# One Strassen step in the input projections of a hybrid attention and state-space layer

## The chip, the cores and the metric

The kernel runs on one core of one Trainium2 chip, as a single launch. The metric is its device time in microseconds (us). Three runs of the kernel before were timed, and one further execution was recorded by the hardware profiler. A difference between two kernels is the ratio of such times.

## The reference, cut to what matters

One layer is computed for a new stream of 2048 tokens and for 32 sample tokens that continue another stream. All data are fp32, the model width is 1024.

```python
h = _rms_norm(x, pre_norm_w)
proj = h @ w_in                       # 1024 x 9760 columns
q, k, v, g_att, z, xbc, dt_raw, gate_a, gate_s = _split_cols(proj)
q, k = rope(q), rope(k)
att = windowed attention of q, k, v with sinks
branch_a = (att * silu(g_att)) @ w_attn_o
xs, bm, cm = split(silu(causal_dwconv(xbc, conv_buf, conv_w, conv_b)))
dt = softplus(dt_raw + dt_bias)
y, h_new = chunked state-space scan of xs, dt, bm, cm from state h0   # the state is carried on
yz = y * silu(z)
yz = group-wise RMS norm of yz, 4 groups of 512
branch_s = yz @ w_ssm_o
merged = sigmoid(gate_a) * branch_a + sigmoid(gate_s) * branch_s
out = x + _rms_norm(merged @ w_out, post_norm_w)
```

The columns of `w_in` are 1024 for q, 256 each for k and v, 1024 for the attention gate, 2048 for z, 3072 for x, B and C (the input of the convolution), 32 for dt, and 1024 for each of the two merge gates.

## The kernel before

The 2048 tokens are worked through in four blocks of 512; block 1 also takes the 32 sample tokens, 544 in all. Activations lie transposed, channels on the 128 partitions and tokens along the row, so a projection's result tile is 128 output channels by the block's tokens.

**A job.** One job is one such tile of one projection. The weight tile (1024 x 128) is split into two fp32r parts, hi (ScalarE copies it, L131) and lo (VectorE subtracts hi from the weight, L135), and so are the activations (`hhi`, `hlo`, made in `stage_a`, L262 and L263). A job adds up 24 matmuls (L151): for each of 8 slices of 128 input channels hi x hi, hi x lo and lo x hi, each 512 columns in one PSUM bank, or two times 272 in block 1. The PSUM pool `mm` has four banks for this. A function `evac` of the job then takes the result from PSUM.

**The weights.** In block 0 each weight tile is read, split, and the two parts are kept in DRAM (`wd`, L137); blocks 1 to 3 read them from there (L126). `prep` runs two jobs ahead of the matmuls (`LOOK`), loads in block 0 four (`LOOK_DMA`). The tiles of the pool `wp` hold them.

**Order.** The jobs of a block are listed in a fixed order: dt; then for each of the four groups of the scan four tiles of x, one each of B and C, four of z, and the state projection (`ssm_out`, 8 half-length jobs) of the group two before it, which stands between x and B; then K, V, and Q and attention gate in turns, 8 + 8 merge gate tiles, the attention's output projection and the output. Four stages can be told apart in block 0: scan 30 to 395 us, attention 395 to 560, merge gates 560 to 660, output projections to 755. Block 1 runs from 755 to 1535, block 2 from 1540 to 2279 (its scan stage to 1935), block 3 to 3006.

**Side work.** What isn't a projection is a list of steps: scan chunks, norms, attention units, the next block's `stage_a`. One step is issued per full job (the counter `units_`), so that its instructions stand between matmuls in TensorE's queue. A job may name steps that have to be through before it (`need`); they are then issued at once.

**Parts that the change touches.** `evac_conv` (L370 and on) copies a tile from PSUM with a halo (L381), applies four taps, one on ScalarE (L384) and three on VectorE (L387), and SiLU (L393). `silu2` (L402, L403) makes the gate z from PSUM. A chunk of the scan loads its cumulated sums (L422, L425), prepares (decay tile `rr` at L447, `s`, `xh`, `xl` at L461 to L466 on GpSimd and ScalarE) and finishes (L477 to L496; `H` is the carried state, all in SBUF). `squares` and `norm` follow the last chunk. RoPE (L627 to L630), the splits of Q (L699, L700) and of K (L726, L728) into hi and lo, and the scores (L765, L766) are in the attention part. `emit_first` (L154) emits dt and the first two tiles half by half in block 0, so that they start before the second half of the activations is there. All DMAs are issued by SyncE (SP).

## Time and profile before

| | us |
|---|---|
| median of three runs | 3019.72 (3015.81 to 3024.2) |
| profiled execution | 3019.91 |
| its span in the trace | 3018.1 |
| TensorE busy | 2969.7 |
| VectorE busy | 1733.8 |
| ScalarE busy | 1128.8 |
| GpSimd busy | 502.7 |

The profiled execution is 1.8 us longer than its span, and 0.2 us from the median of the runs. The granted clock of TensorE was 0.998 of full speed over the span, which is its upper level of 2.4 GHz. Busy time is that of matmuls (PE), weight loads (PEld) and of the instructions of VectorE (DVE), ScalarE (ACT) and GpSimd (POOL); waits on semaphores are not in it.

### The profile page before, as it was taken

The page shows a single profiled execution, that of the slowest core. Times are in us where ns is not written, and L with a number is a line of the kernel's source. Part 1 is how long each engine was busy: PE and PEld are TensorE (multiplying, and loading weights), DVE is VectorE, ACT ScalarE, POOL GpSimd, SP SyncE. Part 2 cuts the span into 40 slices and gives each one's busy share as a digit, 9 for nine tenths or more (in the row PEclk, how much of TensorE's full clock was granted, in tenths as well). Part 3 has the DMA queues.
Part 4 walks back from the last instruction along what each step waited for, and adds up shares of the span by engine and source line. Part 5 has one row for each costly group of instructions (what it writes and reads, how often), then busy time and mean ns, then how long its engine had stood idle before and what let it go on. Part 6 is the DMA issues. An engine that isn't in the chain of part 4 may idle for free.

```text
span 3018.1 us, 46690 instructions
## 1 busy us (share of the span) xinstructions
PE 2969.7 (98%) x17983; PEld 2527.1 (84%) x17983; DVE 1733.8 (57%) x3722; ACT 1128.8 (37%) x2752; POOL 502.7 (17%) x599
## 2 busy tenths in 40 slices
PE   8999999999999999999999999999999999999998
PEld 7877877788999999999998877887788777887787
DVE  6878777644686756563346745655135766556402
ACT  5655435433454323342124433234123443124311
POOL 1322210001132312000102222200011222110000
PEclk9999999999999999999999999999999999999999
DMA  8977786697756455334557555543657665554454
GB/s 283 286 252 255 265 269 223 207 304 266 230 178 182 148 191 173 140 120 182 203 181 235 178 193 187 189 154 126 216 211 228 201 189 172 192 173 153 156 200 155
DMA packets 306214, 606.99 MB, mean 201 GB/s; under 512 B 21768, under 2 KB 231016, under 8 KB 258888
## 3 DMA queue, kind: packets, MB, share of 16 engines
q1 hardware_dynamic: 305992, 604.00, 60.4%
q8 instruction: 142, 2.33, 0.3%
q14 instruction: 80, 0.66, 0.1%
HBM read 478.86 MB, written 125.09 MB: 200 GB/s over the span
## 4 chain that ended last, share of the span: by engine, by line
PE 56%; DVE 4%; DMA 3%; ACT 2%; issue 1%; POOL 1%; SPq 0%; DVEq 0%; POOLq 0%; ACTq 0%
PE mm L151 49%; DMA rr<-cd 2%; PE sd L804 1%; PE sd L787 1%; PE sd L481 1%; DVE u L387 1%; PE sd L477 1%; PE sd L765 1%; PE sd L485 1%; PE sd L766 1%; ACT rr L450 1%; DMA w<-wd 1%; POOL rr L447 1%; PE sd L446 0%; PE sd L920 0%
## 5 line engine op out<-in xcount | busy, mean ns | idle before, releaser
L151 PE MATMUL mm<-hhi,w 128*128 128x512 f32 (+2 forms) x6160 | 1673.6, 354 | 2.4 <-DMA w<-wd 1.3
L151 PEld LDWEIGHTS mm<-hhi,w 128*128 128x128 f32 x6160 | 1082.6, 188 | 167.0 <-issue 12.1
L151 PE MATMUL mm<-hlo,w 128*128 128x512 f32 (+2 forms) x3104 | 1091.0, 352 | 0.4 <-DVE hlo L263 0.4
L151 PEld LDWEIGHTS mm<-hlo,w 128*128 128x128 f32 x3104 | 586.0, 189 | 75.6 <-DVE hlo L263 0.7
L151 PE MATMUL mm<-u,w 128*128 128x512 f32 (+1 forms) x2880 | 567.6, 353 | 0.2 <-DMA w<-wd 0.2
L151 PEld LDWEIGHTS mm<-u,w 128*128 128x128 f32 x2880 | 467.3, 188 | 76.6 <-issue 2.8
L450 ACT ACTIVATE rr<-rr,ncum 128x128 f32<-128x128 f32 (+1 forms) x544 | 170.0, 386 | 131.7 <-POOL rr L447 131.5
L387 DVE SCALAR_TENSOR_TENSOR u<-xp,par,u 128x512 f32<-128x512 f32 (+1 forms) x240 | 172.8, 743 | 43.9 <-ACT u L384 43.4
L135 DVE TENSOR_TENSOR w<-raw,w 128x1024 fp32r<-128x1024 f32 (+1 forms) x124 | 147.1, 1187 | 64.9 <-ACT w L131 64.4
L151 PE MATMUL mm<-tA,w 128*128 128x512 f32 (+2 forms) x688 | 174.0, 340 | 0.1
L743 ACT ACTIVATE pt<-sd,nm 128x192 f32<-128x192 f32 (+3 forms) x260 | 105.2, 413 | 156.9 <-DVE nm L737 142.1
L889 POOL TENSOR_TENSOR s<-s,S 128x512 f32<-128x512 f32 (+1 forms) x32 | 45.4, 1417 | 636.3 <-DVE s L888 601.6
L131 ACT ACTIVATE w<-raw 128x1024 fp32r<-128x1024 f32 (+1 forms) x125 | 118.5, 948 | 62.5 <-PE mm L151 46.4
L629 POOL TENSOR_TENSOR s<-s,cs 128x512 f32<-128x512 f32 (+1 forms) x40 | 52.7, 1318 | 467.4 <-DVE s L627 467.4
L151 PEld LDWEIGHTS mm<-tA,w 128*128 128x128 f32 x688 | 118.3, 188 | 14.2 <-ACT tA L892 0.3
L888 DVE SCALAR_TENSOR_TENSOR s<-tA,mm 128x512 f32<-128x512 f32 (+1 forms) x40 | 23.4, 584 | 182.7 <-PE mm L151 182.7
L381 ACT COPY xp<-mm 128x512 f32<-128x512 f32 (+1 forms) x120 | 59.1, 493 | 175.9 <-PE mm L151 172.3
L447 POOL TENSOR_SCALAR_AFFINE_SELECT rr<-rr 128x1024 f32<-128x1024 f32 (+1 forms) x68 | 84.1, 1237 | 232.9 <-DMA rr<-cd 207.3
L735 DVE TENSOR_REDUCE mx<-sd 128x2 f32<-128x384 f32 (+3 forms) x140 | 66.0, 511 | 88.7 <-PE sd L766 82.1
L151 PE MATMUL mm<-S,w 128*128 128x512 f32 (+2 forms) x344 | 116.4, 338 | 0.4 <-DVE S L893 0.4
L403 DVE SCALAR_TENSOR_TENSOR u<-s,mm 128x512 f32<-128x512 f32 (+1 forms) x80 | 46.4, 586 | 116.0 <-ACT s L402 116.0
L580 DVE TENSOR_TENSOR S<-S,mm 128x512 f32<-128x512 f32 (+1 forms) x120 | 69.6, 585 | 72.9 <-PE mm L151 72.6
(245 smaller groups left out, 3637.6 us busy)
## 6 DMA issues: line engine op xcount, KB each, us to landing
w<-wd SPq DMA_DIRECT2D x276, 1024.0 KB
wd<-w SPq DMA_DIRECT2D x92, 1024.0 KB
w<-wd SPq DMA_DIRECT2D x99, 512.0 KB
raw<-in_w_in_dram SPq DMA_DIRECT2D x77, 512.0 KB
rr<-cd SPq DMA_DIRECT2D x64, 512.0 KB
wd<-w SPq DMA_DIRECT2D x33, 512.0 KB
ee<-cd SPq DMA_DIRECT2D x128, 128.0 KB
x<-in_x_prompt_dram SPq DMA_DIRECT2D x24, 512.0 KB
```

What stands on the lines that cost most here:

```text
L131: act.activation(hi, src, AF.Copy)
L135: vec.tensor_tensor(lo, src, hi.bitcast(F32), op=ALU.subtract)
L151: last_mm[0] = pe.matmul(ps, w[:, k, :], r(k, n0, n), start=k == 0 and i == 0, stop=k == kt - 1 and i == len(ops) - 1)
L381: act.copy(xp[:, 3 + n0:3 + n0 + m], ps[:, :m])
L387: vec.scalar_tensor_tensor(o[:, d0:d0 + n], xp[:, off + t:off + t + n], convw[:, t, ci:ci + 1], o[:, d0:d0 + n], op0=ALU.mult, op1=ALU.add)
L403: vec.scalar_tensor_tensor(o[:, n0:n0 + n], t[:, n0:n0 + n], 1.0, ps, op0=ALU.add, op1=ALU.mult)
L447: pl.affine_select(w[:q, :, :q], w[:q, :, :q], pattern=[[0, 8], [1, q]], compare_op=ALU.is_ge, fill=-1e30, base=0, channel_multiplier=-1)
L450: act.activation(w[:q, h, :q], w[:q, h, :q], AF.Exp, scale=1.0, bias=ncum[:q, co + g * 8 + h:co + g * 8 + h + 1])
L580: vec.tensor_tensor(s[:, n0:n0 + n], s[:, n0:n0 + n], ps, op=ALU.add)
L629: pl.tensor_tensor(sh[:, :tb], sh[:, :tb], cs[:, 1, :tb], op=ALU.mult)
L735: vec.tensor_reduce(mx[:, cols], src, axis=AX.X, op=ALU.max)
L743: act.activation(dst, src, AF.Exp, bias=nm[:, i:i + 1], scale=0.125, accum_out=den[:, i:i + 1])
```

## The change

Two neighbouring 128-column tiles of an input projection become one pair. The 1024 input channels are cut in two halves (A11, A12 are the pair's first column tile, A21, A22 its second), and the tokens of the block in two halves (B11, B21 the two channel halves of the first tokens, the others of the second). One Strassen step in Winograd's form makes the four result tiles from seven products in place of eight. Each product is 4 channel slices x 3 matmuls (hi x hi, hi x lo, lo x hi) of 256 columns, 272 in block 1. 38 pairs a block take this path; the state projection, the attention output and the output projection stay as they are.

- **Activations:** `stage_a` makes the sums t1 to t4 beside the block's B11, B21 and B22 (`sums_a`, `sums_b`, `sums_c`) and splits all of them.
- **Weights:** three of a pair's seven weight pieces are blocks of the weight itself, loaded and split in every block (in block 0 the subtraction is on VectorE, in blocks 1 to 3 on GpSimd). The other four are sums, added on GpSimd in block 0, split on VectorE and kept in DRAM. `wp` has nine slots for pieces and four for raw blocks; `supply` runs eight pieces ahead.
- **Results:** `emit_pair` takes each product from PSUM into the two result tiles in SBUF: products 0 and 4 by a ScalarE copy, the other five by VectorE, with two half-width sums on GpSimd behind product 4. Convolution, SiLU, RoPE and gates then read SBUF.
- **dt** is five half-block products of 8 matmuls, and `emit_first` is gone.
- **z** goes to DRAM (`zd`) and is read back and multiplied on behind the scan, in `squares`, which is now two steps on its own.
- **The carried state** goes through DRAM between blocks (`hstate`); the pool `u` has 2 tiles, not 5, `rr` 2, not 3.
- **Q and K** stay plain fp32 for the scores, four matmuls a unit on row halves.
- **Side work** advances two steps a pair (`tick`), and the state projection comes ahead of the group's x.

Lines that only rename, `add_entries`, `group`, `spread`, and the changes to RoPE and the output of blocks 0 to 2 are left out here.

```diff
-LOOK = 2
-LOOK_DMA = 4
+NW = 9
+NR = 4
...
-    wp = pool("wp", 3)
+    wp = pool("wp", NW)
     hp = pool("hp", 1)
-    up = pool("up", 5)
+    up = pool("up", 2)
     sp = pool("sp", 8)
     s2 = pool("s2", 6)
+    xq = pool("xq", 2)
...
-    hhi = hp.tile([P, KT, UW], F32R, name="hhi")
-    hlo = hp.tile([P, KT, UW], F32R, name="hlo")
+    HN = UW // 2
+    hb = {n: hp.tile([P, 2, HK, HN], F32R, name=n) for n in ("b11", "b21", "b22", "t1", "t2", "t3", "t4")}
+    hstate = [wdram.tile([P, 512], F32, name=f"hst{g}") for g in range(4)]
...
+    def load_raws():
+        while rawnext[0] < min(len(rawlist), rawdone[0] + NR):
+            i = rawnext[0]
+            view, k0, c0 = rawlist[i]
+            r = wp.tile([P, HK * P], F32, name="raw", bufs=NR)
+            dma(r.rearrange("p (k c) -> p k c", k=HK), view[:, k0:k0 + HK, c0:c0 + P])
+            rawtiles[i] = r
+            rawnext[0] += 1
+
...
+    def halves(w, src, eng):
+        act.activation(w[:, 0], src, AF.Copy)
+        eng.tensor_tensor(w[:, 1], src, w[:, 0].bitcast(F32), op=ALU.subtract)
...
+        if not first and kind != "pure":
+            n = 1 if kind == "mix" else 2
+            dma(w[:, :n].bitcast(F32), held[e % per_block[0]])
             return
...
+        elif kind == "plain":
+            halves(w, rawtiles[en["raw"]], vec)
+            keep(e, w)
+            raw_free()
+        elif not first:
+            halves(w, rawtiles[en["raw"]], pl)
+            raw_free()
         else:
-            vec.tensor_tensor(lo, src, hi.bitcast(F32), op=ALU.subtract)
-        held[j] = wdram.tile([P, used.shape[1]], F32, name=f"wd{j}")
-        dma(held[j], used.bitcast(F32))
+            r11, r21, r22, r12 = (rawtiles.get(en["raw"] + i) for i in range(4))
+            pos = en["pos"]
+            if pos == 0:
+                halves(w, r11, vec)
+            elif pos == 1:
+                s1 = s2.tile([P, UW], F32, name="s2")[:, :HK * P]
+                pl.tensor_tensor(s1, r21, r22, op=ALU.add)
+                pl.tensor_tensor(r21, r21, r11, op=ALU.add)
+                pl.tensor_tensor(r11, r11, s1, op=ALU.add)
+                en["s1"] = s1
+                halves(w, r11, vec)
+                keep(e, w)
+            elif pos == 2:
+                halves(w, r12, vec)
+                pl.tensor_tensor(r12, r12, r11, op=ALU.add)
+                raw_free()
...
+            elif pos == 4:
+                halves(w, entries[e - 3]["s1"], vec)
+                keep(e, w)
+            elif pos == 5:
+                halves(w, r22, vec)
+                raw_free()
...
+    def supply():
+        while nalloc[0] < min(len(entries), nused[0] + NW - 1):
+            alloc(nalloc[0])
+            nalloc[0] += 1
...
+    def emit_dt(j):
+        jb = jobs[j]
+        n = jb["tb"] // 2
+        e0, e1 = jb["entries"]
+        res = []
+
+        def run():
+            for n0, ops in ((0, ((e0, "b11"), (e1, "b21"))), (n, ((e0, "t3"), (e0, "b22"), (e1, "b22")))):
+                ps = mm.tile([P, 512], F32, name="mm")[:, :n]
+                for i, (e, h) in enumerate(ops):
+                    yield from group(ps, e, moving(h, n), 0, n, i == 0, i == len(ops) - 1)
+                res.append((ps, n0, n))
+        spread(run(), 5 * HK * 2)
+        used(2)
+        jb["evac"](res)
+
+    def emit_pair(j, between):
+        jb = jobs[j]
+        tb = jb["tb"]
+        n = tb // 2
+        es = jb["entries"]
+        y0, y1 = jb["dest"]()
+        first, second = slice(0, n), slice(n, tb)
+
+        def run(which):
+            for i in which:
+                ps = mm.tile([P, 512], F32, name="mm")[:, :n]
+                name = ("b11", "t2", "b21", "t3", "t1", "t4", "b22")[i]
+                yield from group(ps, es[i], moving(name, n), 0, n, True, True)
+                used(1)
+                if i == 0:
+                    act.copy(y0[:, first], ps)
+                elif i == 1:
+                    vec.tensor_tensor(y0[:, second], ps, y0[:, first], op=ALU.add)
+                elif i == 2:
+                    vec.tensor_tensor(y0[:, first], ps, y0[:, first], op=ALU.add)
+                elif i == 3:
+                    vec.tensor_tensor(y1[:, first], ps, y0[:, second], op=ALU.subtract)
+                elif i == 4:
+                    act.copy(y1[:, second], ps)
+                    pl.tensor_tensor(y0[:, second], y0[:, second], y1[:, second], op=ALU.add)
+                    pl.tensor_tensor(y1[:, second], y1[:, first], y1[:, second], op=ALU.subtract)
+                elif i == 5:
+                    vec.tensor_tensor(y1[:, first], ps, y1[:, first], op=ALU.add)
+                elif i == 6:
+                    vec.tensor_tensor(y0[:, second], ps, y0[:, second], op=ALU.add)
+        spread(run((0, 1, 2)), 9 * HK)
+        between()
+        spread(run((3, 4, 5, 6)), 12 * HK)
+        for f, y in zip(jb["evac"], (y0, y1)):
+            f(y)
...
+    def add_pair(view, c1, c2, tb, dest, evacs, **kw):
+        a11, a12, a21, a22 = ((view, k0, c) for c in (c1, c2) for k0 in (0, HK))
+        es = add_entries("pure", [a11, None, a12, None, None, a22, None], [a11, a21, a22, a12])
+        new_job(dict(kind="pair", entries=es, tb=tb, dest=dest, evac=evacs, **{k: list(v) if k != "name" else v for k, v in kw.items()}))
...
+            def sums_a():
+                r = st["rawh"]
+                if b > 0:
+                    parts("b11", "b11")
+                vec.tensor_tensor(r["b11"], r["b11"], r["t1"], op=ALU.subtract)
+                vec.tensor_tensor(r["t1"], r["t1"], r["b22"], op=ALU.subtract)
+
+            def sums_b():
+                r = st["rawh"]
+                parts("t3", "t1")
+                if b > 0:
+                    parts("b22", "b22")
+                    parts("b21", "b21")
+                vec.scalar_tensor_tensor(r["b22"], r["b11"], -1.0, r["b22"], op0=ALU.mult, op1=ALU.subtract)
+
+            def sums_c():
+                r = st["rawh"]
+                parts("t1", "b11")
+                vec.tensor_tensor(r["b21"], r["b22"], r["b21"], op=ALU.add)
+                parts("t2", "b22")
+                parts("t4", "b21")
...
+        def conv_dest():
+            t = st["xp"] = xq.tile([P, 2, UW + 6], F32, name="xq")
+            return t[:, 0, 3:3 + tb], t[:, 1, 3:3 + tb]
...
+        def evac_z(g, f):
+            def go(y):
+                silu2(y)
+                if ("zd", g) not in st:
+                    st["zd", g] = dram.tile([P, 4, UW], F32, name="zd")
+                dma(st["zd", g][:, f, :tb], y)
             return go
+
+        def silu2(y):
+            t = s2.tile([P, UW], F32, name="s2")
+            act.activation(t[:, :tb], y, AF.Tanh, scale=0.5)
+            vec.scalar_tensor_tensor(y, t[:, :tb], 1.0, y, op0=ALU.add, op1=ALU.mult)
...
+                        if b == 0:
+                            pl.memset(h, 0.0)
+                        else:
+                            dma(h, hstate[g])
...
-                    r = ph.tile([P, 8, P], F32, name="rr", bufs=3)
+                    r = ph.tile([P, 8, P], F32, name="rr", bufs=2)
...
-            steps += [[load(0), load(1)], [], [prp(0)], [prp(1), load(2)], [],
-                      (zdone, [fin(0), CUT, prp(2), load(3)]), [fin(1), CUT, prp(3)]]
+            zt = {}
+
+            def zload(f0):
+                def go():
+                    for f in (f0, f0 + 1):
+                        zt[f] = s2.tile([P, UW], F32, name="s2")
+                        dma(zt[f][:, :tb], st["zd", g][:, f, :tb])
+                return go
+
+            def squares(f0):
+                def go():
+                    x2 = st["x2", g]
+                    for f in (f0, f0 + 1):
+                        vec.tensor_tensor(x2[:, f, :tb], x2[:, f, :tb], zt[f][:, :tb], op=ALU.mult)
+                        act.activation(zt[f][:, :tb], x2[:, f, :tb], AF.Square)
+                        if f:
+                            acc = st["sq", g]
+                            pl.tensor_tensor(acc[:, :tb], acc[:, :tb], zt[f][:, :tb], op=ALU.add)
+                        else:
+                            st["sq", g] = zt[f]
+                return go
+            steps += [[load(0), load(1)], [], [prp(0)], [prp(1)], [],
+                      [fin(0), load(2), CUT, prp(2)], [fin(1), load(3), CUT, prp(3)], []]
             if smp:
-                steps[-1].append(load(4))
-            steps.append([fin(2)] + ([CUT, prp(4)] if smp else []))
-            steps.append([fin(3)])
-            if smp:
-                steps.append([fin(4)])
-
-            def squares():
-                x2 = st["x2", g]
-                acc = None
-                for f in range(4):
-                    sq = s2.tile([P, UW], F32, name="s2")
-                    act.activation(sq[:, :tb], x2[:, f, :tb], AF.Square)
-                    if acc is not None:
-                        pl.tensor_tensor(acc[:, :tb], acc[:, :tb], sq[:, :tb], op=ALU.add)
-                    else:
-                        acc = sq
-                st["sq", g] = acc
+                steps += [[fin(2), load(4), CUT, prp(4)], [fin(3)], [], (zdone, [fin(4), zload(0)])]
+            else:
+                steps += [[fin(2)], (zdone, [fin(3), zload(0)])]
+            steps += [[squares(0), zload(2)], [squares(2)]]
...
-            steps[-1].append(squares)
-            return steps, [[], [], [norm], [], [apply]]
+            return steps, [[norm], [], [apply]]
...
+                            pe.matmul(ss[par][:, e * 192 + lo[e]:e * 192 + 192],
+                                      qs[h, (2 * p + e) * P:(2 * p + e + 1) * P],
+                                      kk[h, p * P + e * 64 + lo[e]:p * P + e * 64 + 192], start=True, stop=True)
...
-            proj(C_X + g * 512, 4, [bk["evac_conv"](g * 4 + f, (lambda f=f, ux=ux: ux()[:, f, :])) for f in range(4)],
-                 need=[f"n{b}.{g - 2}"] if g >= 2 else [])
+            ux = unit(bk, ("x2", g))
             if g >= 2:
                 ssm_out(g - 2)
-            proj(C_X + 2048 + g * P, 1, [bk["evac_conv"](16 + g, bctile(bk, ("b2", g)))],
-                 need=[f"o{b - 1}"] if g == 0 else [], pre=[open_phase("ssm", b)] if g == 0 else [])
+            for f in (0, 2):
+                pair(C_X + g * 512 + f * P, C_X + g * 512 + f * P + P, bk["conv_dest"],
+                     [bk["evac_conv"](g * 4 + f + i, i, (lambda k=f + i, ux=ux: ux()[:, k, :])) for i in range(2)])
             scan, nrm = bk["ssd_steps"](g, ph)
-            proj(C_X + 2560 + g * P, 1, [bk["evac_conv"](20 + g, bctile(bk, ("c2", g)))], need=["dt"],
+            pair(C_X + 2048 + g * P, C_X + 2560 + g * P, bk["conv_dest"],
+                 [bk["evac_conv"](16 + g, 0, bctile(bk, ("b2", g))), bk["evac_conv"](20 + g, 1, bctile(bk, ("c2", g)))],
+                 need=["dt"] + ([f"o{b - 1}"] if g == 0 else []), pre=[open_phase("ssm", b)] if g == 0 else [],
                  after=[(f"s{b}.{g}", scan, (f"n{b}.{g}", nrm))])
-            proj(C_Z + g * 512, 4, [bk["silu2"]((lambda f=f, uu=uu: uu()[:, f, :])) for f in range(4)], name=("z", b, g))
+            for f in (0, 2):
+                pair(C_Z + g * 512 + f * P, C_Z + g * 512 + f * P + P, bk["z_dest"],
+                     [bk["evac_z"](g, f + i) for i in range(2)], name=("z", b, g))
...
+    def tick():
+        for side in list(active):
+            advance(side)
...
+        if jb["kind"] == "pair":
+            tick()
+            emit_pair(j, tick)
+        elif jb["kind"] == "mix":
+            emit_dt(j)
+            if j == 0:
+                derive_first()
+        else:
+            units_ += len(jb["entries"]) / 2
+            while units_ >= 1.0:
+                units_ -= 1.0
+                tick()
```

## Rows read from the trace of the kernel before

**Rows 1.** The page's first part: busy us, share of the span, instructions.

```profile
PE 2969.7 (98%) x17983; PEld 2527.1 (84%) x17983; DVE 1733.8 (57%) x3722; ACT 1128.8 (37%) x2752; POOL 502.7 (17%) x599
```

**Rows 2.** Waits of TensorE: us in total, times, longest us.

```profile
PE sd L259 <- DVE xn L255: 11.4, 1, 11.4
PE sd L477 <- DVE H L496: 7.4, 9, 2.3
```

**Rows 3.** Busy us of each engine (instructions) in five stages; clock, DMA share, GB/s.

```profile
core 0: us, PE busy (x) PEld busy (x) DVE busy (x) ACT busy (x) POOL busy (x), PEclk, DMA share, GB/s
30.00:395.00 365.00, 360.82 (x1882) 291.82 (x1880) 297.70 (x477) 189.07 (x373) 103.16 (x111) 1.00 0.83 269
395.00:560.00 165.00, 162.84 (x900) 128.93 (x902) 124.34 (x289) 82.97 (x222) 15.61 (x15) 1.00 0.70 230
560.00:660.00 100.00, 100.00 (x500) 79.64 (x499) 41.78 (x88) 37.32 (x71) 0.28 (x1) 1.00 0.84 275
755.00:1160.00 405.00, 401.10 (x3302) 387.98 (x3301) 273.73 (x592) 168.29 (x458) 105.89 (x165) 1.00 0.59 185
1540.00:1935.00 395.00, 391.71 (x2076) 319.88 (x2075) 250.23 (x491) 145.12 (x329) 90.94 (x114) 1.00 0.61 195
```

**Rows 4.** The same for 100 to 200 us.

```profile
100.00:200.00 100.00, 97.38 (x536) 78.20 (x535) 92.62 (x143) 58.63 (x126) 36.93 (x40) 0.98 0.78 238
```

**Rows 5.** Timeline of TensorE, 512 columns: start us, us, the instruction.

```profile
400.56 0.40 PE L151 MATMUL mm<-hlo,w 128*128 128x512 f32 x1
...
408.92 0.40 PE L151 MATMUL mm<-hlo,w 128*128 128x512 f32 x1
```

**Rows 6.** Timeline of TensorE in block 1, 272 columns.

```profile
1001.06 0.29 PE L151 MATMUL mm<-hlo,w 128*128 128x272 f32 x1
...
1009.00 0.28 PE L151 MATMUL mm<-hlo,w 128*128 128x272 f32 x1
```

**Rows 7.** Timeline of TensorE in the last output tiles, 256 columns.

```profile
2989.30 0.28 PE L151 MATMUL mm<-S,w 128*128 128x256 f32 x1
...
2998.40 0.28 PE L151 MATMUL mm<-S,w 128*128 128x256 f32 x1
```

**Rows 8.** Timeline of VectorE: two instructions in a row, 512 elements.

```profile
108.35 0.68 DVE L492 TENSOR_TENSOR u<-u,ee 128x512 f32<-128x512 f32 x1
108.96 0.68 DVE L496 TENSOR_TENSOR H<-H,sd 128x512 f32<-128x512 f32 x1
```

**Rows 9.** Groups of VectorE by form: busy us, mean ns, idle before and releaser.

```profile
L580 DVE TENSOR_TENSOR S<-S,mm 128x272 f32<-128x272 f32 x48 | 20.3, 436 | 30.1 <-PE mm L151 29.9
```

**Rows 10.** Timeline of VectorE and GpSimd, 100.89 to 104.5 us.

```profile
100.89 0.74 DVE L387 SCALAR_TENSOR_TENSOR u<-xp,par,u 128x512 f32<-128x512 f32 x1
...
101.55 1.22 DVE L135 TENSOR_TENSOR w<-raw,w 128x1024 fp32r<-128x1024 f32 x1
...
102.02 1.90 POOL L466 TENSOR_TENSOR xl<-s,xh 128x512 fp32r<-128x512 f32 x1 [0.97 <-ACT xh L465]
...
102.68 1.79 DVE L387 SCALAR_TENSOR_TENSOR u<-xp,par,u 128x512 f32<-128x512 f32 x1
```

**Rows 11.** Single lines: count, ns min/median/max, first and last start.

```profile
L387 DVE SCALAR_TENSOR_TENSOR u<-xp,par,u x240: 239/746/1790, 34.5 to 2553.5; 128x512 f32<-128x512 f32 x119, 128x32 f32<-128x32 f32 x1
L135 DVE TENSOR_TENSOR w<-raw,w x124: 677/1222/2346, 16.7 to 732.1; 128x1024 fp32r<-128x1024 f32 x92, 128x512 fp32r<-128x512 f32 x32
L466 POOL TENSOR_TENSOR xl<-s,xh x68: 1270/1295/2207, 77.1 to 2636.1; 128x512 fp32r<-128x512 f32 x64, 32x512 fp32r<-32x512 f32 x4
L461 POOL TENSOR_TENSOR s<-xd,te x68: 1031/1043/1957, 73.9 to 2634.3; 128x512 f32<-128x512 f32 x64, 32x512 f32<-32x512 f32 x4
```

**Rows 12.** Groups of GpSimd by form, 60 to 395 us.

```profile
L447 POOL TENSOR_SCALAR_AFFINE_SELECT rr<-rr 128x1024 f32<-128x1024 f32 x16 | 19.9, 1242 | 40.9 <-DMA rr<-cd 40.9
```

**Rows 13.** Timeline of TensorE: a chunk's end between two matmul streams.

```profile
1706.32 1.05 PE L477 MATMUL sd<-c,H 128*128 128x128 f32 x8
...
1709.12 0.39 PE L151 MATMUL mm<-hhi,w 128*128 128x512 f32 x1
```

**Rows 14.** A single line: the evacuation of dt.

```profile
L309 ACT ACTIVATE s<-mm,dtb x5: 479/679/684, 30.4 to 2282.7; 32x512 f32<-32x512 f32 x3, 32x272 f32<-32x272 f32 x2
```

**Rows 15.** The page's costliest groups: the weight loads of the projections.

```profile
L151 PEld LDWEIGHTS mm<-hhi,w 128*128 128x128 f32 x6160 | 1082.6, 188 | 167.0 <-issue 12.1
```

587 lines of the change are left out of this document (294 added, 293 removed).

## The prediction, made before the change was built

> **What bounds the kernel now.** I read the page first, then the engine's waits, then busy time by stage. TensorE is busy 2969.7 of 3018.1 us [rows 1], and its waits on other work are small: no single wait of it is over 11.4 us, and the largest that recurs is 2.3 us on the carried state [rows 2]. So the kernel is TensorE's length, and a change must either shorten what TensorE does or lengthen what it waits for. The stages differ in what stands close behind: in block 0's scan stage (30 to 395 us) VectorE is busy 297.7 of 365 us and the DMA engines 0.83, in block 2's (1540 to 1935) 250.2 of 395 and 0.61 [rows 3]. In 100 to 200 us VectorE is busy 92.6 of 100, the densest row that the trace has for it [rows 4].
>
> **What it removes: 12 of 96 matmul columns in each pair.** Starts in the three timelines give the time of one matmul in a stream. 512 columns: 36 matmuls from 400.56 to 408.92, 0.232 us [rows 5]. 272 columns: 63 from 1001.06 to 1009.00, 0.126 us [rows 6]. 256 columns: 78 from 2989.30 to 2998.40, 0.1167 us [rows 7]. So halving the columns halves the time. A pair of column tiles was 2 x 24 matmuls of 512, 11.15 us, and becomes 7 x 12 of 256, 9.80 us: 1.35 us saved. In block 1, 96 of 272 (12.10 us) become 84 (10.58 us): 1.51 us saved. A block has 38 pairs, 20 in the scan stage and 18 behind it. TensorE's saving is 27 us in block 0's scan stage, 24 us in the rest of block 0, 51 us in each of blocks 2 and 3 and 57 us in block 1: 210 us in all, if nothing else ends later.
>
> The Trainium skill ("TensorE: Matmul & The Clock Gate", Back-to-back issue gap) speaks against this: it gives 81 ns for one matmul of a weight-load and matmul stream at 128 columns and 131 ns at 512. On a straight line between them that is an estimate of 98 ns at 256, and a pair would rise from 48 x 131 = 6.3 us to 84 x 98 = 8.2 us. The rows above have 232 and 117 ns in place of that, so they decide.
>
> **What it adds on VectorE and GpSimd.** Per pair: 7 results to take from PSUM (2 copies on ScalarE, 5 on VectorE) and 2 half-width GpSimd sums. In block 0 also 7 splits of 512 elements on VectorE (before: 2 of 1024) and 4 GpSimd sums of 512; in blocks 1 to 3 3 splits whose subtraction is on GpSimd. A VectorE instruction of 512 occupies 0.60 us, start to start [rows 8], one of 272 from PSUM 0.44 us less that overlap, 0.36 [rows 9]; a split of 1024 takes 1.13 us, 101.55 to 102.68 [rows 10]; a GpSimd one of 512 takes 1.29 us [rows 11].
>
> These cannot all run side by side. At 102.02 us GpSimd's subtraction takes 1.90 us, not 1.29: it begins under a VectorE split that ends at 102.77. VectorE's next instruction with two SBUF inputs then takes 1.79 us, not 0.75, until GpSimd is through [rows 10]. The medians and maxima say the same: 0.746 against 1.790 us for that line [rows 11]. Its maximum is the median and one GpSimd instruction more. So a VectorE instruction with two SBUF inputs and a GpSimd instruction exclude each other, and their times add.
>
> The Trainium skill ("SBUF — State Buffer", Who interferes with whom) calls this one locked port pair, held for a whole instruction. By that rule the trace agrees. Without it only VectorE's own time would count in block 0's scan stage.
>
> *Block 0's scan stage.* Time that excludes itself, per pair: 7 x 0.60 + 4 x 1.29 + 2 x 0.65 (half of 1.29, estimated) = 10.7 us, already over TensorE's 9.8. Twenty pairs: 214 us. The convolution (12 pairs, each 2 x (3 x 0.66 + 0.60)): 62. The 16 chunks (GpSimd 1.24 [rows 12], 1.04 and 1.29 [rows 11], VectorE 2 x 0.60): 76. Squares, the gate z and the norm, per group 3 on GpSimd and 12 on VectorE: 4 x 11.1, 45. SiLU of z, now from SBUF: 10. Splits for the state projection: 14. Sum 421 us, against 365 that the stage takes now. At the 0.926 of rows 4 it is 455: **+90 us** where TensorE alone would give -27. From below: without exclusion VectorE has 297.7 + 20 x (5 x 0.36 + 7 x 0.60) - 40 x 1.13 = 373 us, +8; from above, at 0.85, 495 us, +130. I take 455, since rows 10 show the exclusion in both directions.
>
> *Rest of block 0.* TensorE saves 24. The eight gate pairs (560 to 660) have 8 x 11.3 = 90 us of excluding work on 78 us of matmuls, so I give back 10: **-14**. The attention stretch has slack (VectorE 124.3 of 165 [rows 3]).
>
> *Blocks 1 to 3.* TensorE: **-160 us**. Excluding work in block 2's scan stage: 20 x (3 x 1.29 + 1.3) + 62 + 76 + 45 + 10 = 297 us of 368, 81%. It fits as a sum but not everywhere: two convolution pairs with two chunk ends and a set of squares have 20.8 + 2.4 + 6.3 = 29.5 us of it on 19.6 + 2 x 2.8 us of matmuls (a chunk end from 1706.32 to about 1709.1 [rows 13]), 4.3 too much, and the state projection between them needs half of its time. The supply runs 8 weight pieces ahead, 8 x 1.40 = 11.2 us, which levels some of this. Also PSUM: four banks of 12 matmuls leave 3 x 1.40 = 4.2 us to take a result away, where four of 24 left 16.7. The trace has no row for so short a time. From below 0; from above 4.3 us in each of eight stretches (convolution and gate pairs of four groups), 34 a block. I take 20, over the middle because nothing levels PSUM: **+60**.
>
> **Steps that are forced.** The scan of a group is 12 slots now (14 in block 1), and K's first pair needs the last group's whole scan: 8 turns come first, so four slots are emitted at once, one before. Behind them on TensorE's queue stand K's matmuls, and K's first copy waits until the scan's tiles are free. The state projection of group 0 comes with 14 turns for 15 slots (17 in block 1), so the normalisation, or its DRAM round trip too, stands ahead of its matmuls. A recurring wait of this sort was 2.3 us at longest [rows 2], and a chunk's VectorE chain (about eight instructions of 0.6) is some 4 us. From 10 (both mostly hidden) to 70 us; I take 7 a block and 2 more for block 1: **+30**.
>
> **Start, dt, attention scores.** Before, dt and two tiles were done at 30.4 us [rows 14]. Now the second half of dt waits for a sum of activations, and the second product for two more, each split once: five instructions of 1024 on VectorE (1.22 us [rows 11]) with ScalarE copies between, some 8 us behind the last transposes, and then a pair of 9.8: **+15** (8 to 20). Dt: 40 x 0.117 against 16 x 0.232, 1 us a block: **+4**. Scores: 8 matmuls of 192, under 0.117 us each, become 4 in plain fp32, which are two passes (8 records for 4 matmuls; 8 in 1.05 us at 128 columns, 0.11 a pass [rows 13]), so 8 x 0.165 by columns, or half of it where two row halves run at once: +0.4 or -0.2 us for each of 64 units, -14 to +29. I take **+5**.
>
> **DMA.** A pair reads 4 x 512 KB of sums and 3 x 256 KB of raw weights, 2.88 MB against 2.10. Block 2's scan stage: 195 GB/s x 395 us = 77 MB, and 16 for this, 8 for z and 2 for the state: 103 MB in 368 us, 280 GB/s, where full share would be 185 / 0.59 = 314 [rows 3]. Costed at nothing while the 11.2 us of lead cover it. SP issues 7 or 8 transfers a pair, not 2 to 4, at some 0.4 us: 3 of 9.8 us.
>
> **Sum.** 90 - 14 - 160 + 60 + 30 + 15 + 4 + 5 = +30 us. The profiled execution took 3019.9 us (span 3018.1 and 1.8 around it), 0.2 from the median: **3050 us**.
>
> **Rivals.**
> *Faster: the lead levels the crowding.* If weight pieces made ahead in the quiet state projections carry the crowded pairs, blocks 1 to 3 lose 30 us instead of 60, the forced steps 15, block 0's stage +65, its rest -20, start 10 and scores -5: 3020 - 61 = 2959. It decides once blocks 1 to 3 lose together, crowding and forced steps, under 60 us. For it: TensorE's small waits today. Against: rows 10. Chance 0.31.
> *PSUM is freed too late.* If one result of each convolution pair waits 3 us too long behind VectorE, and one of each other pair 1 us, blocks 1 to 3 lose 36 x 3 + 24 = 132 instead of 60: 3122. For it: 4.2 us against 16.7. Chance 0.15.
> *DMA becomes the bound.* A group without a state projection moves 20.1 MB (5 pairs, chunks 3.1, z 2.1, state 0.5) in some 63 us of TensorE time. At the 275 GB/s of 560 to 660, the highest of rows 3, it takes 73, 10 more in two groups of three blocks: 3110. Against: the share there is 0.84, not 1. Chance 0.11.
> *The weight load sets the pace*, so that the change shortens nothing: at its recorded 188 ns [rows 15] a pair would take 15.8 us, and the time would pass 3500. Rows 7 speak against it. Chance 0.01.
> The forecast has 0.42.
>
> **Range and chances.** Under 0.3% (9 us) a change cannot be told from none here. The forecast's own range is 3015 to 3090. The whole reaches from 2945, which leaves out the far end of the first rival, to 3150, past the PSUM case. Faster: most of the first rival and nothing else, 0.30. Within 0.3%: 0.08, where the first rival and the forecast meet. Slower: 0.62.
>
> **What would show it.** Block 0's scan stage near 455 us (dt to K), with VectorE over 85% busy, GpSimd over 50%, and TensorE waiting on split weights; a pair at 9.8 us in the gate stretches of blocks 2 and 3; TensorE's waits in the scan stages of blocks 1 to 3 on PSUM takers and on weights; K's start a few us late. It is wrong if block 0's stage stays under 400 us, or if the scan stages of blocks 2 and 3 fall below 375 us.

## The result, and the profile after

The changed kernel took 3485.92 us (median of 4 runs, 3480.94 to 3491.07), the kernel before 3019.42: ratio 1.154, 95% interval 1.152 to 1.157. It is 466 us slower. The forecast was 3050, its range ended at 3150. The profiled execution has a span of 3482.8 us.

Stages, from the first projection matmul of each to the first of the next (starts in the timelines), us before and after. Here the attention stage goes from K to the end of group 3's state projection, and the gate stage has the second half of Q and attention gate and the 16 merge gate tiles. By these starts block 0's stages began at 15, 381, 476 and 653 us before, and block 2's scan stage took 361 us (1555 to 1916), not the 395 of its window in [rows 3].

| | scan | attention | gates | output | block |
|---|---|---|---|---|---|
| block 0 | 365.5, 515.6 | 95.5, 152.5 | 177.0, 201.4 | 95.4, 95.0 | +231 |
| block 1 | 403.9, 475.6 | 104.7, 131.7 | 194.3, 196.0 | 103.6, 100.1 | +97 |
| block 2 | 360.8, 423.4 | 92.1, 111.7 | 176.1, 173.1 | 94.5, 92.3 | +77 |
| block 3 | 366.6, 417.6 | 92.7, 113.4 | 176.1, 163.3 | 104.1, 104.5 | +59 |

The page's first part answers [rows 1], and below it stands the row of the granted clock in 40 slices from its second part.

```profile
PE 2993.9 (86%) x21655; PEld 2736.8 (79%) x21655; DVE 2317.4 (67%) x4548; ACT 1417.8 (41%) x3343; POOL 1452.8 (42%) x1424
...
PEclk8889988999999889999999989999999989999999
```

TensorE is busy no less than before, although it has fewer columns to do, and it is idle 3482.8 - 2993.9 = 489 us, where it was 48. The clock row gives the reason for the first: the mean granted clock is 0.928, so for 3482.8 x 0.072 x 2 = some 500 us it was at its lower level, 1.2 GHz. In the timeline a matmul of 256 columns takes 118 ns at the upper level (median of 8421 starts) and 213 at the lower (of 913). TensorE was busy in 364 us of the stretches at the lower level (the trace's clock records laid over its timeline), which lost 364 x (1 - 118/213) = 162 us.

What TensorE waited for, answering [rows 2] (us in total, times, longest us):

```profile
PE sd L735 <- POOL s L718: 59.4, 16, 9.2
PE mm L206 <- ACT w L124: 56.3, 14, 11.1
PE mm L206 <- DVE xq L294: 53.6, 21, 5.8
PE mm L206 <- ACT v L757: 46.9, 6, 13.1
PE mm L206 <- ACT xq L300: 27.4, 15, 4.7
PE mm L206 <- ACT s L300: 20.4, 4, 7.0
...
PE mm L206 <- ACT xq L292: 13.0, 5, 7.4
```

Added up over the view by kind: engines that take a product from PSUM ("takers", L292 to L306) 177 us, the norm behind a scan (its sum of squares, L718, 59, the normalised activations, L757, 48), split weights (L124, L125) 61, weights from DRAM 5, other side work 128, 477 in all. No one of them explains the result.

One tile of 5.6 us stood in the gate stages before and stands in the attention stages now. The stages, answering [rows 3]:

```profile
30.00:531.00 501.00, 377.94 (x2531) 344.67 (x2532) 419.52 (x659) 226.80 (x476) 245.88 (x228) 0.87 0.62 206
531.00:684.00 153.00, 113.19 (x735) 100.75 (x734) 116.78 (x202) 56.56 (x136) 64.53 (x52) 0.84 0.60 202
...
1883.00:2307.00 424.00, 361.61 (x2612) 335.09 (x2611) 302.83 (x564) 176.17 (x402) 199.96 (x206) 0.92 0.73 230
...
3215.00:3378.00 163.00, 159.43 (x1414) 147.15 (x1411) 91.96 (x247) 79.64 (x226) 69.41 (x60) 1.00 0.67 223
```

VectorE (third busy column) and GpSimd (fifth) together are busy 665 us in the 501 of block 0's scan stage, 181 in the 153 of its attention stage, 503 in the 424 of block 2's scan stage. This is more than the work alone, since the time for which one of the two holds up an instruction of the other counts as busy. Only in the last row, block 3's gates, does the pair work as it should: full clock and hardly a stop.

One stop in block 2's scan stage, from the timeline of all engines:

```profile
2209.43 1.36 POOL L636 TENSOR_SCALAR_AFFINE_SELECT rr<-rr 128x1024 f32<-128x1024 f32 x1 [6.11 <-DMA ee<-cd]
...
2210.82 2.45 ACT L639 ACTIVATE rr<-rr,ncum 128x128 f32<-128x128 f32 x8 [8.88 <-POOL rr L636]
...
2215.28 0.35 ACT L300 COPY xq<-mm 128x256 f32<-128x256 f32 x1
...
2215.69 2.62 PE L206 MATMUL mm<-t,w 128*128 128x256 f32 x12 [1.96 <-ACT xq L300]
...
2216.43 0.74 POOL L302 TENSOR_TENSOR xq<-xq 128x256 f32<-128x256 f32 x1
...
2217.20 0.43 DVE L304 TENSOR_TENSOR xq<-mm,xq 128x256 f32<-128x256 f32 x1 [7.36 <-POOL xq L302]
...
2218.51 6.46 DVE L562 SCALAR_TENSOR_TENSOR u<-xq,par,u 128x512 f32<-128x512 f32 x5 [0.55 <-ACT u L553]
...
2219.66 1.75 POOL L125 TENSOR_TENSOR w<-raw,w 128x512 fp32r<-128x512 f32 x1
...
2221.97 1.79 POOL L125 TENSOR_TENSOR w<-raw,w 128x512 fp32r<-128x512 f32 x1
...
2224.89 0.41 DVE L294 TENSOR_TENSOR xq<-mm,xq 128x256 f32<-128x256 f32 x1
...
2225.36 2.16 PE L206 MATMUL mm<-t,w 128*128 128x256 f32 x12 [2.22 <-DVE xq L294]
```

GpSimd waits 6.11 us for a load of the scan (L636), ScalarE 8.88 us for GpSimd's decay tile (L639), and its copy of the fifth product (L300) stands behind that; TensorE stops for 1.96 us until the copy has freed a bank. VectorE sits idle for 7.36 us, because the sixth product's taker (L304) needs GpSimd's half-width sum (L302), which needs that copy. Then five convolution taps take 6.46 us in place of five times 0.74, while GpSimd runs weight splits beside them. The next product's taker (L294) stands behind the taps, and TensorE stops for 2.22 us until a bank is free. ScalarE's waits for the decay tile are not new (152.8 us in 55 times, before 131.5 in 57); what is new is that a result in PSUM can wait 4.2 us, not 16.7, by the prediction's sum. And after a stop the clock falls. Here is the longest of that stage, the stretch that follows it and a later one (the granted clock is the column before the last two: 0.51 and 1.00):

```profile
2061.54 10.74 PE L206 MATMUL mm<-v,w 128*128 128x512 f32 x36 [8.64 <-ACT v L757]
```

```profile
2062.00:2066.00 4.00, 4.00 (x10) 2.74 (x10) 3.21 (x5) 1.96 (x4) 2.35 (x1) 0.51 0.81 322
2072.00:2090.00 18.00, 18.00 (x117) 14.97 (x116) 10.52 (x21) 8.09 (x22) 6.78 (x7) 1.00 0.61 173
```

### The profile page after: what moved, and what is told of

The parts are those of the page before. It is cut to its first block, busy times and chain, and to the rows that moved or that the text cites. A ratio compares the mean times of both kernels' runs of the same rounds, so it can differ in the third digit from the quotient of the medians.

```text
span 3482.8 us, 59784 instructions
## 1 busy us (share of the span) xinstructions
PE 2993.9 (86%) x21655; PEld 2736.8 (79%) x21655; DVE 2317.4 (67%) x4548; ACT 1417.8 (41%) x3343; POOL 1452.8 (42%) x1424
## 5 line engine op out<-in xcount | busy, mean ns | idle before, releaser
L206 PE MATMUL mm<-t,w 128*128 128x256 f32 (+1 forms) x7328 | 1054.6, 299 | 199.8 <-ACT w L124 56.3
L206 PEld LDWEIGHTS mm<-t,w 128*128 128x128 f32 x7328 | 982.3, 202 | 234.1 <-ACT w L124 59.5
L206 PE MATMUL mm<-b,w 128*128 128x256 f32 (+1 forms) x5600 | 813.6, 298 | 46.6 <-DVE xq L294 10.2
L125 POOL TENSOR_TENSOR w<-raw,w 128x512 fp32r<-128x512 f32 x342 | 484.0, 1417 | 801.8 <-ACT w L124 711.8
L206 PEld LDWEIGHTS mm<-b,w 128*128 128x128 f32 x5600 | 755.4, 201 | 71.1 <-issue 17.0
L124 ACT ACTIVATE w<-raw 128x512 fp32r<-128x512 f32 x634 | 389.6, 627 | 469.2 <-PE mm L206 234.8
L206 PE MATMUL mm<-v,w 128*128 128x512 f32 (+1 forms) x2240 | 511.3, 361 | 48.0 <-ACT v L757 46.9
L206 PEld LDWEIGHTS mm<-v,w 128*128 128x128 f32 x2240 | 381.0, 194 | 113.0 <-ACT v L757 48.1
L125 DVE TENSOR_TENSOR w<-raw,w 128x512 fp32r<-128x512 f32 x292 | 227.2, 799 | 64.3 <-ACT w L124 62.9
L639 ACT ACTIVATE rr<-rr,ncum 128x128 f32<-128x128 f32 (+1 forms) x544 | 168.7, 384 | 152.8 <-POOL rr L636 152.8
L562 DVE SCALAR_TENSOR_TENSOR u<-xq,par,u 128x512 f32<-128x512 f32 x192 | 182.3, 975 | 16.3 <-ACT u L553 15.8
L206 PE MATMUL mm<-u,w 128*128 128x512 f32 (+1 forms) x640 | 169.0, 352 | 0.0
L636 POOL TENSOR_SCALAR_AFFINE_SELECT rr<-rr 128x1024 f32<-128x1024 f32 (+1 forms) x68 | 78.2, 1151 | 184.2 <-DMA rr<-cd 153.4
L206 PEld LDWEIGHTS mm<-u,w 128*128 128x128 f32 x640 | 112.3, 188 | 17.0
L304 DVE TENSOR_TENSOR xq<-mm,xq 128x256 f32<-128x256 f32 (+1 forms) x80 | 34.1, 427 | 117.4 <-POOL xq L302 117.3
```

Source lines behind the costliest of these rows:

```text
L124: act.activation(w[:, 0], src, AF.Copy)
L125: eng.tensor_tensor(w[:, 1], src, w[:, 0].bitcast(F32), op=ALU.subtract)
L206: last_mm[0] = pe.matmul(ps, a[:, k, :], r(k, n0, n), start=start and k == 0 and i == 0, stop=stop and k == HK - 1 and i == len(ops) - 1)
L562: vec.scalar_tensor_tensor(o[:, d0:d0 + n], src[:, t:t + n], convw[:, t, ci:ci + 1], o[:, d0:d0 + n], op0=ALU.mult, op1=ALU.add)
L636: pl.affine_select(w[:q, :, :q], w[:q, :, :q], pattern=[[0, 8], [1, q]], compare_op=ALU.is_ge, fill=-1e30, base=0, channel_multiplier=-1)
L639: act.activation(w[:q, h, :q], w[:q, h, :q], AF.Exp, scale=1.0, bias=ncum[:q, co + g * 8 + h:co + g * 8 + h + 1])
```

## The experiments

Theories: **queues** (results and weights are late because VectorE, GpSimd and ScalarE wait for one another in order, and the first two shut each other out), **PSUM** (four banks of 1.4 us are too few, whatever the takers do), **steps** (forced side work and the norm), and, over all, **clock** (a stop costs more than its length).

**Clock, by itself.** Two kernels are the kernel before with 32 stops put in (`k` copies, 4 or 14):

```diff
+        act.copy(t[:, :8], ps[:, :8])
+        for i in range(1, k):
+            act.copy(t[:, i * 8:i * 8 + 8], t[:, i * 8 - 8:i * 8])
+        with tc.issue_after(last_mm[0].ins):
+            last_mm[0] = pe.matmul(ps[:, 8:16], ident, t[:, k * 8 - 8:k * 8], start=True, stop=True)
```

In both kernels the matmuls of the merge gate tiles are also held to their written order, so the two are compared with each other first.

> The kernel before, and in the middle of each of the 32 merge gate tiles of gate S TensorE waits once for a chain of 4 small ScalarE copies behind its own last matmul, about 1.0 to 1.5 us. Nothing else is changed. A stop that only costs its length: 32 x 1.2, 3050 to 3070. If such short stops already lower the clock: 3100 or more.

> The same with a chain of 14 copies, about 3 to 4 us a stop. A stop that only costs its length: 32 x 3.5, 3120 to 3150. Clock theory (each is followed by 3.4 to 10 us at half clock, as behind the waits of the changed kernel): 32 x 1.7 to 5 us more, 3180 to 3290, with the granted clock near 0.5 to 0.7 in the gate stretches.

They took 3067.0 and 3193.0 us. Short stops, the waits of TensorE and block 2's gate stretch:

```profile
PE sd L189 <- ACT stop L187: 31.1, 32, 2.0
```

```profile
2165.00:2275.00 110.00, 109.06 (x490) 88.64 (x489) 26.01 (x61) 18.82 (x35) 10.34 (x8) 1.00 0.59 210
```

Long stops, the same with block 0's gate stretch too:

```profile
PE sd L189 <- ACT stop L187: 105.2, 32, 5.0
```

```profile
540.00:655.00 115.00, 87.11 (x443) 68.83 (x442) 44.76 (x118) 56.44 (x201) 0.00 (x0) 0.88 0.50 160
2165.00:2275.00 110.00, 84.17 (x409) 66.41 (x408) 24.76 (x83) 42.97 (x174) 0.00 (x0) 0.86 0.34 111
```

Short stops of 0.94 us (median) left the clock at 1.00. With 3.23 us a stop, TensorE was idle 105.2 - 31.1 = 74 us more, but the time rose by 126: 52 us, 1.6 us a stop, went to a clock of 0.86 to 0.88. So the clock theory is shown, with its price, which is at the low end of what was expected; the clock fell less than expected too. The Trainium skill ("TensorE: Matmul & The Clock Gate", HAM oscillation — how this bites in real kernels) reckons such a loss as half of the time at the lower clock. For the first stretch, 8 stops, that is an estimate of 115 x 0.12 = 13.8 us, 1.7 a stop; the measured 1.6 agrees.

**Queues, one edit each on the changed kernel.** Split weights from DRAM for the unsummed pieces too:

```diff
-        if not first and kind != "pure":
+        if not first:
...
-        elif not first:
-            halves(w, rawtiles[en["raw"]], pl)
```

> Blocks 1 to 3 read the three unsummed weight pieces of a pair from DRAM as parts, kept there in block 0, so that their ScalarE copies and GpSimd subtractions (342 of 1.42 us, 484 us in the changed kernel) are gone. Queue theory (TensorE waits for results that stand behind GpSimd's and ScalarE's queues, and each wait of 2 to 3 us is followed by half clock): blocks 1 to 3 lose 25 to 40 us each less, block 0 the same or up to 10 us worse for 57 MB more writes; total 3385 to 3420. PSUM theory (a bank of 1.4 us is too short whatever the other engines do) and step theory (the scan's and the norm's forced steps): under 20 us in all, 3465 to 3490.

3396.5 us, 89 less, as the queue theory had it. TensorE's waits on takers fell from 177 to 95 us. Blocks 1 to 3 gained 48, 43 and 31 us. Block 0 lost 35 (expected: at most 10): TensorE's waits on split weights, now all in block 0, rose from 61 to 103 us. The three more writes a pair are the likely reason, which is not shown. And weights from DRAM now make TensorE wait, 44.9 us where it was 4.8:

```profile
PE mm L206 <- ACT w L124: 98.1, 21, 10.8
...
PE mm L206 <- DMA w<-wd: 44.9, 16, 6.6
```

The two half-width sums on VectorE:

```diff
-                    pl.tensor_tensor(y0[:, second], y0[:, second], y1[:, second], op=ALU.add)
-                    pl.tensor_tensor(y1[:, second], y1[:, first], y1[:, second], op=ALU.subtract)
+                    vec.tensor_tensor(y0[:, second], y0[:, second], y1[:, second], op=ALU.add)
+                    vec.tensor_tensor(y1[:, second], y1[:, first], y1[:, second], op=ALU.subtract)
```

> The two half-width sums behind a pair's fifth product are on VectorE in place of GpSimd. Queue theory: VectorE's take-up of the sixth product no longer waits for GpSimd (30.2 us in block 2's scan stage, 19.3 and 11.9 in block 0's), so the waits of TensorE on results (some 110 us) fall by half, and with the clock 60 to 90 us are gained: 3395 to 3425. Theory that VectorE's own time is the bound in block 0: block 0 gets slower by 2 x 40 x 0.3 = 10 to 25 us, the rest the same: 3480 to 3510.

3431.2 us, 55 less, 11 to 16 us in every block: a smaller gain than the queue theory's range had. VectorE's waits for the sum (117.3 us) are gone and more work on VectorE made all blocks faster, block 0 too. But TensorE's waits on takers, which were to fall by half, are 171 us where they were 177. The gain is spread over other waits (33 us in all) and the clock, so this run does not show that the half-width sums were what made the takers late.

Block 0's weight sums on VectorE (in four lines `pl.tensor_tensor` becomes `vec.tensor_tensor`):

> Block 0's four weight sums of a pair are on VectorE (0.6 us each by the rows of before) in place of GpSimd (1.29 and more). Exclusion theory (VectorE with two SBUF inputs and GpSimd shut each other out, so their times add): 38 pairs x 4 x 0.7 us less of excluding work, 50 to 100 us gained in block 0, 3385 to 3435. Theory that VectorE alone is full in block 0 (419.5 of 501 us): 38 x 4 x 0.6 = 91 us more on the full engine, 3520 to 3575. Theory that the raw weight blocks arrive late (GpSimd's first sum waits 61.5 us for them): within 15 us of 3486.

3415.2 us, 71 less, 60 of it in block 0. VectorE's busy time in block 0's scan stage hardly rose (419.5 to 425.3 us) though it had 80 sums of 0.6 us more to do, since its other instructions became shorter. Of its taps (L562) the mean fell from 898 to 751 ns. The exclusion theory holds, the theory that VectorE alone is full falls, and so does that of late raw blocks. The Trainium skill ("SBUF — State Buffer", Who interferes with whom) has the two engines share one exclusive port pair, and by that rule this trace agrees once more.

The write of a split piece three pieces later, so that SyncE's queue does not wait for the split (`write_kept(e - LATE if first else e)` ahead of each `alloc`):

> In block 0 the write of a split weight piece to DRAM is issued three pieces later, so that SyncE's queue no longer stands behind the split (180.8 us of waits there in block 0's scan stage) and the raw loads behind it go out early. Raw loads late are the cause of block 0's waits on split weights (47.5 us of TensorE): block 0 gains 40 to 100 us, 3385 to 3445. Exclusion of VectorE and GpSimd is the cause: under 20 us, 3465 to 3490.

3467.0 us, 19 less, although SyncE's waits on splits in block 0's scan stage fell from 180.8 to 75.7 us. TensorE's waits on split weights there fell from 47.5 to 35.3 us. But SyncE then waited longer for raw slots (77.7 us on GpSimd's sums, 38.9 before), and GpSimd still waited 42.6 us for raw blocks (61.5 before). So the order of the writes is worth some 20 us; what the late loads cost in all this run alone does not tell.

**PSUM.** Two products in one bank; and five banks for products, three for the side work:

```diff
+                    if i % 2 == 0:
+                        bank["t"] = mm.tile([P, 512], F32, name="mm")
+                    ps = bank["t"][:, (i % 2) * n:(i % 2) * n + n]
```

```diff
-    mm = pool("mm", 4, space=bass.MemoryType.PSUM)
-    sd = pool("sd", 4, space=bass.MemoryType.PSUM)
+    mm = pool("mm", 5, space=bass.MemoryType.PSUM)
+    sd = pool("sd", 3, space=bass.MemoryType.PSUM)
```

> In blocks 0, 2 and 3 two products in a row share one PSUM bank, so that the four banks hold up to eight results. PSUM theory: nearly all of TensorE's waits on results (some 110 us, and half of that again by the clock) go in these blocks: 3340 to 3390. Queue theory: the results are taken late because the takers wait for something else; the depth helps with the short ones: 20 to 50 us, 3435 to 3465. Step theory: under 10 us.

> The changed kernel with five PSUM banks for the products and three, not four, for the side work. PSUM theory (a result is taken too late for four banks of 1.4 us): TensorE's waits on takers (some 110 us, and half as much by the clock) fall by a third or more, 3420 to 3460. Queue theory (the takers are late by 3 to 7 us, more than one bank): within 15 us of 3486. The side work misses its fourth bank: slower, 3500 or more.

3530.3 and 3524.9 us, both slower, which the PSUM theory did not allow. In the first TensorE waits more often for the taker of a pair's first product (46.4 us, 25 times, in place of 13.0, 5 times). Most of these waits stand ahead of the second product, which writes the other half of that bank, so this run says nothing of depth. In the second, waits on takers fall from 177 to 94 us, so depth does count, but the rest grows, and with four banks or five the waits come to 477 and 493 us. The side work has lost a bank, as its own expectation had it (3500 or more), so depth without that loss is not measured:

```profile
PE mm L206 <- ACT w L124: 87.7, 19, 11.7
PE sd L735 <- POOL s L718: 73.0, 16, 13.9
PE mm L206 <- ACT v L757: 52.5, 6, 15.0
```

**Steps.** More turns, and an empty step ahead of the norm:

```diff
-            return steps, [[norm], [], [apply]]
+            return steps, [[], [norm], [], [apply]]
...
+            units_ += 1.0 if jb.get("one") else len(jb["entries"]) / 2
```

> More turns of the side work: three a pair in group 1 and in group 3's gate pairs, one for each job of the state projection before K, and one empty step between the squares and the norm. Nothing else changes. Step theory: TensorE's waits on the norm (the squares' sum 59.4 us, the normalised activations 46.9, the root 13.7) fall by two thirds, 80 us, and 40 more by the clock: 3360 to 3400. Queue theory: denser steps crowd VectorE and GpSimd more, so under half of that comes back: 3430 to 3480.

3429.6 us, 56 less. (The 13.7 us of the root are waits of dt's sums, L532, behind another norm on VectorE; they do not belong to this one.) The wait on normalised activations went (46.9 us to 0.9) and that on the squares fell to 33.1, but nearly all the gain is in the attention stages (11 to 24 us each); the scan stages stay within 11 us of what they were. That the denser steps crowd the same engines there would explain it, but is not shown.

**Together.** The first, second and step edits; then with the weight sums and the late writes as well:

> Three single edits together: unsummed weights read as parts in blocks 1 to 3, the two half-width sums on VectorE, more turns. Alone they gave 90, 55 and 56 us. If each removes stops of its own, and each stop costs its clock, the gains add up or better: 3285 or less. If they remove the same stops, or the denser turns only move waits: 3330 to 3380. If the end is then set by the DMA (552 KB more of transfers a pair in the pure pieces than in the changed kernel, TensorE's waits on weights from DRAM 18.3 us in block 2's scan stage in the run of the first edit): 3310 to 3350 with those waits over 20 us a block.

> Five edits together: unsummed weights read as parts, the half-width sums and the weight sums on VectorE, more turns, the late writes. The three alone gave 189 us together, the weight sums 71. If the gains add, 3225 or less, and 3150 to 3220 where the late writes also pay. Blocks 1 to 3 stay at some 730 to 740 us each (the waits that are left are those on weights from DRAM and on the norm), block 0 over 830. Still slower than before by over 3%, since block 0's splits and sums alone are more VectorE work than its matmuls last.

3296.6 and 3209.6 us: 189 of 200 (a little short of the 3285 for gains that add up), and 276 of 290, so the gains nearly add up, and the edits remove mostly different stops. (By the sizes of the transfers the three unsummed pieces are 3 x 256 = 768 KB more a pair, not 552.) Blocks 1 to 3 are then at 813, 730 and 748 us (before: 807, 724, 740), block 0 at 902 (before: 733).

**How many pairs?** In three kernels with the same edits and seven weight slots a tile that is not in a Strassen pair is computed plainly, as two halves of 256 columns with `b12` kept beside `b11`, `b21` and `b22`. They have twelve pairs a block (behind the last state projection), none, and eighteen (from K on).

```diff
+                yield from group(ps, e0, moving(h0, n), 0, n, True, False)
+                yield from group(ps, e1, moving(h1, n), 0, n, False, True)
...
+            (add_pair if bk["st"].get("seven") else add_classic)(w_in, c1, c2, tb, dest, evacs, **kw)
```

> Strassen only where no scan runs beside it: the twelve pairs behind the last state projection (Q and gate of the second half, the 16 merge gate tiles); the other 26 pairs are two plain tiles of 48 matmuls of 256 columns. The edits of the last run are in it, seven weight slots in place of nine. If the scan beside the pairs is what makes Strassen lose, its scan stages come back to those of before (365, 404, 361, 367 us), the gate stages keep 12 to 16 us a block, and the whole is 2970 to 3010, under the kernel before. If z by DRAM, the smaller pools and the extra copies cost as much as the pairs did: 3040 to 3100. If Strassen's takers or weights are too slow even there: gate stages of 175 us or more.

> The last kernel with no Strassen pair at all: all 76 tiles a block are plain, two halves of 24 matmuls of 256 columns, and the sums of activations and weights are left out. What stays of the change is z and the carried state by DRAM, the smaller pools, one more ScalarE copy a tile, plain fp32 scores, split weights in pieces. If these surroundings cost as much as the twelve-pair kernel has over before (80 us) plus what the pairs save there (48 pairs x 1.35 = 65 us): 3140 to 3170. If the sums and takers of the twelve pairs are part of its loss: 3060 to 3130. If the surroundings are free and all loss is Strassen's: 3020 to 3050.

> The twelve-pair kernel with Strassen from K on as well, eighteen pairs a block. TensorE's saving is 24 x 1.35 = 32 us more. Where the takers fit beside the attention units: 3065 to 3095. Where block 0's attention stretch crowds VectorE (sums and splits of six more pairs) and stops TensorE, with its clock: 3100 to 3140.

The kernel without any pair took 3123.2 us (ratio to before 1.0343, interval 1.0326 to 1.0360), that with twelve 3100.9 (1.0262, 1.0245 to 1.0279), eighteen 3098.7 (1.0259, 1.0244 to 1.0274), all 38 (above, nine slots) 3209.6. The twelve-pair kernel missed its 2970 to 3010: its scan stages, without a pair in them, are 395, 431, 384 and 392 us, not those of before. Block 0's and block 2's scan stage and block 2's gates, without any pair and with all:

```profile
15.00:411.00 396.00, 373.41 (x2848) 348.30 (x2849) 316.48 (x547) 204.43 (x434) 96.33 (x112) 0.98 0.84 276
1606.00:1988.00 382.00, 366.90 (x2870) 342.78 (x2870) 247.29 (x489) 145.77 (x329) 83.12 (x106) 1.00 0.71 218
2087.00:2261.00 174.00, 174.00 (x1565) 162.99 (x1559) 68.22 (x212) 68.85 (x199) 5.85 (x6) 1.00 0.51 158
```

```profile
16.00:505.00 489.00, 389.19 (x2607) 348.67 (x2608) 448.07 (x816) 238.85 (x506) 104.03 (x109) 0.90 0.82 282
1730.00:2111.00 381.00, 347.33 (x2641) 321.61 (x2641) 301.95 (x626) 145.36 (x345) 90.38 (x106) 0.97 0.88 300
2207.00:2368.00 161.00, 159.28 (x1412) 147.18 (x1412) 95.65 (x271) 61.94 (x194) 7.81 (x6) 1.00 0.81 268
```

In block 2's gates twelve pairs save 12 of the 16.2 us that the columns make. In block 2's scan stage twenty pairs take 20 us off TensorE's busy time and give all of it back in stops and clock (0.97). In block 0's they cost 94 us (396.2 to 489.9 by the starts). Over the kernel, from none to all 38: blocks 1 to 3 gain 55 us, block 0 loses 142. From twelve pairs to eighteen blocks 1 to 3 gain 27 and block 0 loses 19, so the whole stays the same within its intervals. And with no pair at all the surroundings (z and state by DRAM, smaller pools, one more copy a tile, plain fp32 scores, halves of 256 columns) cost 103 us, as much as the scan stages grow by (22 to 31 us each); half of it is busy time of TensorE (3022.1 us, before 2969.7), half idle. These runs don't part the surroundings. So of the 466 us the five edits take back 276, some 86 are what the 38 pairs still cost, and some 103 are there without any pair. No version here beats the kernel before.

## Why the prediction was wrong, step by step

- **What it removes: nearly right.** 118 ns a matmul where 117 was forecast. With the short pauses of a stream (starts up to 0.5 us apart, upper clock) the means are 121 ns at 256 columns and 128 at 272, against 235 and 127 before at 512 and 272. By these the columns save some 178 us of the 210.
- **The clock: a term that was not in the sum.** 162 us. [Rows 3] have 1.00 everywhere, and that was taken as given; but it was granted to a TensorE that hardly ever stopped. Every wait of the sum should have been charged at up to one and a half times its length.
- **Block 0's scan stage, +90, and start, +15: mechanism right, size short.** It became +150. The signs that were named are there: VectorE is busy 84% of the stage, GpSimd 49%, and TensorE's largest wait in it is on split weights (47.5 us). Exclusion is shown by the weight sums' run, and with all five edits the pairs still cost 94 us here. The half clock accounts for 41 of the missing 45 (92.4 us busy at the lower clock, by 95/213).
- **Rest of block 0, -14: failed.** It became +81. The attention stretch was waved through for VectorE's slack in the row of before, although its six pairs bring the same sums and splits; their demand was never added up there. Busy time of the two, with what they stretch each other by, comes to 181 us on 153. The gates, charged with 10 us, came out 24 longer.
- **Blocks 1 to 3, -160 + 60 + 30 + 9: failed, +233.** The step that failed is "I take 20" for the crowding. The sum counted VectorE and GpSimd in one account and left ScalarE out, and a sum of demands under 100% says nothing of in-order queues in which a copy, a sum and a taker on three engines wait for each other. It was too favourable as well: the 81% are 297 of 368 us, from a window of 395, but the stage took 361 by its starts, so 297 of some 334, 89%. The splits of unsummed weights alone, on ScalarE and GpSimd, cost 122 us in these blocks, and without them TensorE's waits on takers halve; the half-width sums cost 36.
- **Forced steps, +30: too small.** More turns gave 56 us back. It was overlooked that the norm lost both empty steps ahead of it, so that its matmul stands in TensorE's queue until GpSimd has added the squares (59.4 us).
- **Costed at nothing: z by DRAM and the other surroundings.** The run without any pair puts them, in its form, at 103 us.
- **The rivals.** PSUM freed too late is part of it (177 us of waits on takers, 94 with a fifth bank), but a fifth bank taken from the side work gained nothing in time. DMA shows as waits on weights only when the unsummed pieces are read as parts (33 to 45 us). The lead of eight pieces did not level the crowding: it runs ahead with weights, and the largest waits are on takers. What the prediction named as its disproof, block 2's scan stage under 375 us, was missed in the other direction (423 us); since the stage took 361 before by its starts, the forecast's own change would have left it there.

## What to carry to other kernels

In a kernel like this one, with TensorE busy 98%, work taken off TensorE is paid by whoever prepares operands and takes results: add up the demand of each engine, and of engines that exclude each other, in every stage anew, not only where a row of before is already full, and follow the new dependencies around their in-order queues. Charge a stop of TensorE of some 3 us at one and a half times its length, and measure the surroundings of an idea (layout, buffers, round trips) without the idea.

## What the runs showed of the hardware that was not expected

- Stops of 0.94 us left TensorE's clock at its upper level, stops of 3.23 us brought 0.86 to 0.88 over a stretch with one stop in about 13 us, and cost 1.6 us each beside their length.
- VectorE's takers with a PSUM operand did not stretch under GpSimd (405 to 443 ns over 80 instructions, median 416), while its convolution taps with SBUF inputs went from a median of 744 ns to 2181 at most; single rows of the changed kernel:

```profile
L294 DVE TENSOR_TENSOR xq<-mm,xq x80: 405/416/443, 40.5 to 3064.2; 128x256 f32<-128x256 f32 x60, 128x272 f32<-128x272 f32 x20
```

```profile
L562 DVE SCALAR_TENSOR_TENSOR u<-xq,par,u x192: 732/744/2181, 47.2 to 3035.1; 128x512 f32<-128x512 f32 x192
```

- Moving 80 sums onto the engine that was busy 84% of a stage raised its busy time by 6 us and shortened the stage by 33.
